# A nanmax over 2048 elements: the first tile's load is split by partitions between two issuing engines

## The chip, the cores and the metric

The kernel runs on one core of one Trainium2 chip. The core has five instruction streams that matter here: TensorE (PE), VectorE (DVE), ScalarE (ACT), GpSimd (POOL) and SyncE (SP), and 16 DMA engines that move data between device memory and the on-chip memory of 128 partitions. Time is device microseconds of one execution; the time of a kernel is the median over its runs. A profile is one more execution, recorded by the hardware profiler.

## The reference

```python
batch, seq, dim = 32, 2048, 2048
x = np.random.randn(batch, seq, dim).astype(np.float32)
mask = np.random.rand(batch, seq, dim) < 0.1
x[mask] = np.nan
...
return np.nanmax(x, axis=axis).astype(np.float32)      # axis = -1
```

There are 65,536 rows of 2048 floats, 512 MiB, and one maximum that ignores NaN is wanted of each row: 256 KiB.

## The kernel before

**The arithmetic.** Only the upper 16 bits of each float are changed. A helper `clean` reads them as a signed integer, doubles it, subtracts 0x7F80 and writes it back as an unsigned one, with negative results clipped to zero (`Relu` on ScalarE, the conversion to uint16 on GpSimd). A NaN becomes a pattern that is negative as a float or nearly zero, a small or negative number becomes about zero, and large numbers keep their order. A plain maximum over the row (`tensor_reduce` on VectorE, f32) is then the maximum without the NaNs, as long as it is large enough, and `decode` undoes the step on the 512 results a partition. A count of results that were too small (`mark`, `total`, one small matmul) decides at the very end whether a slow, general version has to run over everything; for this input it doesn't.

**Tiling.** Each partition holds 512 rows. The free dimension is counted in units of 256 elements (`U`), so a row is 8 units (`ROW`). `TILES` lists the tiles; a tile is a list of loads, and a load is a tuple of steps, all in units. A tile of 64 units is 8 rows on each of 128 partitions: 64 KB a partition, 8 MiB. The first two tiles are one load of 16 units (2 MiB) and one of 48 (6 MiB); then come 50 tiles of one 64-unit load each, and then tiles cut into ever smaller loads and steps for a short end.

**Buffers.** There are three buffers of 64 units (`xts`, `BUFS = 3`); tile number n uses buffer n mod 3. A load may be issued when the last reduction of the tile that had the buffer before is done (`free`). The loads of the first three tiles (`AHEAD = 3`) need no buffer freed and are issued at the head of the program, before the barrier at the end of its setup (lines 273 to 286); all others are issued in the main loop. SyncE issues all loads, in the order of tiles. They carry semaphores from 14 lanes in turn (`LANES`); a load also waits for the one that used its lane before.

**Each step.** ScalarE cleans the first half of a step's columns, GpSimd the second half, both as soon as the step's load has landed. The two count on a shared semaphore (`pair`), so VectorE waits once for both and then reduces the rows that are complete. `order.add` writes every instruction with the waits that it still needs: waits that an earlier one on the same engine implies are left out.

**Order on the engines around the change.** SyncE: the three loads ahead, the barrier, then one load after another, each behind its wait for VectorE. ScalarE: the barrier, a table load, one activation on a single column, then the first halves of the steps. GpSimd: four constants, the barrier, the second halves. VectorE: three memsets, then the reductions. At tile numbers in `SETTLE` GpSimd also marks and decodes the rows finished so far.

Of the kernel before, what the change touches and what calls it, by code (L numbers as in the profile page):

```python
# [10 lines left out]
U = 256  # L11
# [2 lines left out]


TILES = (
    [[(16,)], [(48,)]]
    + [[(64,)]] * 50
# [20 lines left out]
OWN = 46  # L39
PAIRS = 6  # L40
# [4 lines left out]
LANES = 14  # L45

AHEAD = 3

# [154 lines left out]
def kernel(  # L203
# [6 lines left out]
    nc = tc.nc  # L210
    P = nc.NUM_PARTITIONS
# [22 lines left out]
    def sbuf(name, shape, dtype):  # L234
        return nc.alloc_sbuf_tensor(name, shape, dtype).ap()

    small = sbuf("small", [P, LEAD // 4], f32)
    xts = [sbuf(f"xt{i}", [P, WIDE * D], i32) for i in range(BUFS)]
# [9 lines left out]
    order = Order(nc)  # L248
    lanes = [[] for _ in range(LANES)]
    issued = 0  # L250

    def load(to, of, deps, own=False):
        nonlocal issued
        turn = issued % LANES
        issued += 1

        def issue():
            inst = nc.sync.dma_start(out=to, in_=of)  # L258
            if own:
                tc.no_tile_sem_insts.add(inst.ins.name)  # L260
            return inst

        e = order.add("sp", nc.sync, issue, deps + lanes[turn], lane=f"load{turn}", step=16)
        lanes[turn] = [e]
        return e

    def source(gi):
        r = P * rows[0] * gi
        return xr[r : r + P * rows[gi]].rearrange("(p s) d -> p (s d)", p=P)
# [3 lines left out]
    ahead = {}  # L273
    base = 0
    for number in range(AHEAD):
        for at, steps in tiles[number]:
            end = at + sum(steps)
            ahead[number, at] = load(
                xts[number][:, at * U : end * U],
                source(0)[:, (base + at) * U : (base + end) * U],  # L280
                [],
                own=True,
            )
        base += sizes[number]
    tc.close()
    tc.compile()  # L286
# [4 lines left out]
    def act(deps, pair=None, **kw):  # L291
        return order.add(
            "act",
            nc.scalar,
            lambda: nc.scalar.activation(**kw),  # L295
            deps,
            lane=pair,
            joint=pair is not None,
        )
# [4 lines left out]
    def pool(deps, do, pair=None, **kw):  # L304
        return order.add(
            "pool", nc.gpsimd, lambda: do(**kw), deps, lane=pair, joint=pair is not None  # L306
        )

    def decode(add, engine, a, b, deps):
        return add(  # L310
            deps,
            engine.tensor_scalar,
            out=halves[:, a:b],
            in0=halves[:, a:b],
            scalar1=float(INF),
            scalar2=0.5,
            op0=ALU.add,
            op1=ALU.mult,
        )

    def clean(by, span, deps, pair):
        to, of = span.bitcast(u16)[:, 1::2], span.bitcast(i16)[:, 1::2]
        if by == "A":
            return act(
                deps, pair, out=to, in_=of, func=ACT.Relu, bias=float(-INF), scale=2.0
            )
        return pool(
            deps,
            nc.gpsimd.tensor_scalar,
            pair,  # L330
            out=to,
            in0=of,
            scalar1=2.0,
            scalar2=float(-INF),
            op0=ALU.mult,
            op1=ALU.add,
        )

    def mark(to, of, deps):
        return pool(  # L340
            deps,
            nc.gpsimd.tensor_scalar,
            out=to,
            in0=of,
            scalar1=NORMAL,
            scalar2=None,
            op0=ALU.is_lt,
        )

    def total(to, of, deps):  # L350
        return act(deps, out=of, in_=of, func=ACT.Relu, bias=0.0, scale=1.0, accum_out=to)
# [11 lines left out]
    for number, loads in enumerate(tiles):  # L363
        if number in (0, SPLIT):
            gi = int(number == SPLIT)
            s = rows[gi]
            xg = source(gi)
            og = outs[r0 : r0 + P * s].rearrange("(p s) -> p s", p=P)
            stores.append([og, accs[:, first : first + s].bitcast(i32)])
            r0 += P * s  # L370
            base = 0
        xt, before = xts[number % BUFS], free[number % BUFS]
        if number in SETTLE:
            to = sum(sizes[: SETTLE[number]]) // ROW
            e_row = done[to - 1]
            e_low = mark(low[:, settled:to], accs[:, settled:to], [e_row])
            e_settled = decode(pool, nc.gpsimd, settled, to, [e_row, e_low])
            settled = to
        if number == len(tiles) - 1:
            assert settled == rows[0]  # L380
            e_early = total(late[:, 0:1], low, [e_low])
        for at, steps in loads:
            end = at + sum(steps)
            e = ahead.get((number, at))
            if e is None:
                e = load(
                    xt[:, at * U : end * U],
                    xg[:, (base + at) * U : (base + end) * U],
                    before,
                )  # L390
            cleaned = []
            a = taken = at
            for i, n in enumerate(steps):
                pair = "pair_%s_%d_%d" % (*e, i) if number >= OWN else f"pair{number % PAIRS}"
                lo, mid, hi = a * U, a * U + n * U // 2, (a + n) * U
                clean("A", xt[:, lo:mid], [e], pair)
                e_clean = clean("P", xt[:, mid:hi], [e], pair)
                cleaned.append((a, a + n, e_clean))
                a += n
                upto = end if a == end else a // ROW * ROW  # L400
                for lo, hi in segments(taken, upto):
                    row = first + (base + lo) // ROW
                    m = max((hi - lo) // ROW, 1)
                    deps = [e for p, q, e in cleaned if p < hi and q > lo]
                    of = lo * U
                    if row >= S - 2:
                        if len(cells) == 1 and e_rest is None:
                            e_rest = dve(
                                [done[S - 3]],
                                nc.vector.tensor_reduce,  # L410
                                out=accs[:, first : S - 2],
                                in_=parts[:, 0 : s - 2],
                                axis=AX.X,
                                op=ALU.max,
                            )
                        if lo % ROW:
                            of -= 1
                            deps.insert(0, cells[row][1])
                        if hi % ROW:
                            to = xt[:, hi * U - 1 : hi * U].bitcast(f32)  # L420
                        else:
                            to = accs[:, row : row + m]
                    elif gi == 1:
                        nth = 0 if lo % ROW == 0 else nth + 1
                        assert nth < PARTS
                        to = parts[:, row - first : row - first + m, nth : nth + 1]
                        deps.append(e_zero)
                    else:
                        assert lo % ROW == 0 and hi % ROW == 0
                        to = accs[:, row : row + m]  # L430
                    e_max = dve(
                        deps,
                        nc.vector.tensor_reduce,
                        out=to,
                        in_=xt[:, of : hi * U]
                        .bitcast(f32)
                        .rearrange("p (c d) -> p c d", c=m),
                        axis=AX.X,
                        op=ALU.max,
                    )  # L440
                    if hi % ROW == 0:
                        for r in range(row, row + m):
                            done[r] = e_max
                    elif row >= S - 2:
                        cells[row] = (hi * U - 1, e_max)
                taken = max(taken, upto)
        free[number % BUFS] = [e_max]
        base += sizes[number]
        if number in (SPLIT - 1, len(tiles) - 1):
            first += s  # L450
# [4 lines left out]
    e = mark(late[:, rows[1] - 1 :], xt[:, p : q + 1 : q - p].bitcast(f32), [e_p, e_q])  # L455
# [7 lines left out]
    e = decode(dve, nc.vector, S - 2, S, [done[S - 2], done[S - 1]])  # L463
# [3 lines left out]
    for og, bits, deps in stores:  # L467
# [6 lines left out]
                lane="store",  # L474
                step=16,
# [66 lines left out]
```

## Time and profile before

| What | Value |
|---|---|
| median of 3 runs | 1246.35 us (1246.26 to 1246.93) |
| the profiled execution's own time | 1246.26 us |
| its span, first to last instruction | 1244.4 us |
| bytes moved by the load and store queue | 537.14 MB, 432 GB/s over the span |
| bytes read from device memory | 536.87 MB |

The span is shorter than the execution's time by what lies before the first and after the last instruction of the program. In the views below, times are microseconds from the start of the span. PE, DVE, ACT, POOL and SPq are the engines, L258 a line of the kernel (a helper's line where the helper records the instruction), `out<-in` the names of what is written and read, followed by shapes and types. A row of the timeline has the start, the duration, the engine, the instruction, and in brackets the idle time before it and what ended it. A row of the waits has who waited for what: total, number of times, the longest. SPq rows are the issues of loads; the page counts DMA work by queue, as a share of the time of all 16 engines.

### The profile page before, as it was taken

Reading aid. Unit: us, or ns where it says so; the run is one execution under the profiler, and the core shown is the slowest. Engines: PE = TensorE matmul, PEld = TensorE weight load, DVE = VectorE, ACT = ScalarE, POOL = GpSimd, SP = SyncE. Lnnn points to the kernel's source line nnn. Section 1 sums busy time; section 2 is a strip of 40 time slices with the busy share of each in tenths; the row PEclk is TensorE's granted clock in tenths of the full one; section 3 lists DMA queues with packets and bytes.
Section 4 is the critical chain, followed back from the end, with each engine's and each line's share of the span. In section 5 each row is a group of like instructions: output and inputs, shape, how many; then the busy total and the mean of one; then the engine's idle time right before and its main releaser. Section 6 shows DMA issues by size and latency. Waiting matters only on the chain.

```text
span 1244.4 us, 572 instructions
## 1 busy us (share of the span) xinstructions
PE 0.2 (0%) x2; PEld 0.1 (0%) x2; DVE 1105.9 (89%) x136; ACT 603.7 (49%) x131; POOL 606.6 (49%) x138
## 2 busy tenths in 40 slices
PE   0000000000000000000000000000000000000000
PEld 0000000000000000000000000000000000000000
DVE  1789889898898988988989889898898999999999
ACT  3354453553534535445354453544535536545556
POOL 3354453543534535445354453544535536545556
DMA  9999999999999999999999999999999999999999
GB/s 404 438 438 438 438 438 438 419 423 438 438 438 438 438 438 430 415 436 438 438 438 438 438 438 421 421 438 438 438 438 438 438 432 419 443 424 430 429 425 375
DMA packets 14688, 537.14 MB, mean 432 GB/s; under 512 B 1760, under 2 KB 1888, under 8 KB 4704
## 3 DMA queue, kind: packets, MB, share of 16 engines
q1 hardware_dynamic: 14688, 537.14, 99.9%
HBM read 536.87 MB, written 0.26 MB: 432 GB/s over the span
## 4 chain that ended last, share of the span: by engine, by line
DMA 50%; DVE 34%; POOL 14%; SPq 2%; issue 0%; ACT 0%; PE 0%
DMA xt<-in_x_dram 50%; DVE acc L302 33%; POOL xt L306 14%; SPq L258 2%; DVE parts L302 1%; POOL late L306 0%; ACT sums L295 0%; PE sums L460 0%; SPq L95 0%
## 5 line engine op out<-in xcount | busy, mean ns | idle before, releaser
L302 DVE TENSOR_REDUCE acc<-xt 128x8 f32<-128x16384 f32 (+5 forms) x95 | 1059.4, 11186 | 134.0 <-POOL xt L306 133.7
L306 POOL TENSOR_SCALAR xt<-xt 128x8192 uint16<-128x8192 int16 (+11 forms) x125 | 602.7, 4836 | 635.0 <-DMA xt<-in_x_dram 635.0
L295 ACT ACTIVATE xt<-xt 128x8192 uint16<-128x8192 int16 (+11 forms) x125 | 601.5, 4839 | 635.2 <-DMA xt<-in_x_dram 635.2
L302 DVE TENSOR_REDUCE parts<-xt 128x1 f32<-128x2048 f32 (+6 forms) x32 | 42.6, 1410 | 0.0
L302 DVE TENSOR_REDUCE xt<-xt 128x1 f32<-128x768 f32 (+1 forms) x4 | 3.7, 944 | 0.0
L302 DVE MEMSET small<- 128x1 f32 x2 | 0.1, 59 | 3.0 <-PEq L286 3.0
L295 ACT ACT_TABLE_LOAD x1 | 1.3, 1283 | 2.9 <-PEq L286 2.9
L306 POOL TENSOR_SCALAR low<-acc 128x312 f32<-128x312 f32 (+2 forms) x3 | 1.9, 626 | 0.2
L306 POOL TENSOR_SCALAR acc<-acc 128x312 uint16<-128x312 uint16 (+3 forms) x4 | 1.4, 343 | 0.3
L295 ACT ACTIVATE sums<-sums 1x22 f32<-1x22 f32 x1 | 0.1, 140 | 1.1 <-PE sums L460 1.1
L295 ACT ACTIVATE low<-low 128x491 f32<-128x491 f32 x1 | 0.6, 585 | 0.0
L460 PE MATMUL sums<-late,small 128*1 128x22 f32 x2 | 0.2, 200 | 1242.4 <-POOL late L306 1242.4
L306 POOL TENSOR_SCALAR late<-acc 128x19 f32<-128x19 f32 x1 | 0.3, 266 | 0.1
L306 POOL TENSOR_SCALAR late<-xt 128x2 f32<-128x2 f32 x1 | 0.2, 218 | 0.1
L460 PEld LDWEIGHTS sums<-late,small 128*1 128x1 f32 x2 | 0.1, 80 | 1242.4 <-issue 1242.4
L523 POOL MEMSET const-float32-0.0<- 128x1 f32 x1 | 0.1, 99 | 0.2 <-issue 0.2
L295 ACT ACTIVATE small<-small 128x1 f32<-128x1 f32 x1 | 0.2, 203 | 0.0
L302 DVE TENSOR_SCALAR acc<-acc 128x2 uint16<-128x2 uint16 x1 | 0.2, 171 | 0.0
L302 DVE TENSOR_REDUCE acc<-parts 128x19 f32<-128x57 f32 x1 | 0.2, 200 | 0.0
L295 ACT ACTIVATION_READ_ACCUMULATOR low<-low 128x1 f32 x1 | 0.2, 187 | 0.0
L295 ACT ACTIVATION_READ_ACCUMULATOR sums<-sums 1x1 f32 x1 | 0.2, 185 | 0.0
L302 DVE MEMSET parts<- 128x63 f32 x1 | 0.1, 111 | 0.0
(3 smaller groups left out, 0.3 us busy)
## 6 DMA issues: line engine op xcount, KB each, us to landing
xt<-in_x_dram SPq DMA_DIRECT2D x2, 7168.0 KB, 30.9
xt<-in_x_dram SPq DMA_DIRECT2D x2, 6144.0 KB, 24.7
xt<-in_x_dram SPq DMA_DIRECT2D x3, 4096.0 KB, 26.7
xt<-in_x_dram SPq DMA_DIRECT2D x5, 2048.0 KB, 34.4
xt<-in_x_dram SPq DMA_DIRECT2D x2, 5120.0 KB, 23.2
xt<-in_x_dram SPq DMA_DIRECT2D x3, 3072.0 KB, 33.6
xt<-in_x_dram SPq DMA_DIRECT2D x4, 1024.0 KB, 34.9
xt<-in_x_dram SPq DMA_DIRECT2D x9, 384.0 KB, 13.9
```

The lines of the kernel that those rows point to most:

```text
L258: inst = nc.sync.dma_start(out=to, in_=of)
L295: lambda: nc.scalar.activation(**kw),
L302: return order.add("dve", nc.vector, lambda: do(**kw), deps)
L306: "pool", nc.gpsimd, lambda: do(**kw), deps, lane=pair, joint=pair is not None
L460: lambda: nc.tensor.matmul(sums, lhsT=ones, rhs=late, start=True, stop=True),
L523: nc = _bacc.Bacc("TRN2", target_bir_lowering=False, num_devices=1)
```

## The change

The first two tiles of 16 and 48 units become one tile of 64 units with one step. Its load is issued in two instructions: partitions 0 to 15 by ScalarE, on ScalarE's own DMA queue, and partitions 16 to 127 by SyncE, 64 KB a partition in both. The loads of the next two tiles are issued by SyncE with all 128 partitions. `load` takes the issuing engine as an argument, and the list of loads that a step waits for can now hold two. Tile numbers behind the first tile are one lower than before.

```diff
--- before.py
+++ after.py
@@ -14,7 +14,7 @@
 
 
 TILES = (
-    [[(16,)], [(48,)]]
+    [[(64,)]]
     + [[(64,)]] * 50
     + [[(24, 40)], [(24, 40)], [(16, 16, 32)], [(8, 16, 32)], [(8, 16, 32)], [(8, 16, 24)]]
     + [[(16, 24)], [(8, 16, 16)], [(16, 16), (16, 16)], [(8, 8, 16), (8, 16)]]
@@ -45,6 +45,7 @@
 LANES = 14
 
 AHEAD = 3
+CORNER = 16
 
 
 
@@ -249,18 +250,19 @@
     lanes = [[] for _ in range(LANES)]
     issued = 0
 
-    def load(to, of, deps, own=False):
+    def load(to, of, deps, own=False, by="sp"):
         nonlocal issued
         turn = issued % LANES
         issued += 1
+        engine = nc.sync if by == "sp" else nc.scalar
 
         def issue():
-            inst = nc.sync.dma_start(out=to, in_=of)
+            inst = engine.dma_start(out=to, in_=of)
             if own:
                 tc.no_tile_sem_insts.add(inst.ins.name)
             return inst
 
-        e = order.add("sp", nc.sync, issue, deps + lanes[turn], lane=f"load{turn}", step=16)
+        e = order.add(by, engine, issue, deps + lanes[turn], lane=f"load{turn}", step=16)
         lanes[turn] = [e]
         return e
 
@@ -275,12 +277,17 @@
     for number in range(AHEAD):
         for at, steps in tiles[number]:
             end = at + sum(steps)
-            ahead[number, at] = load(
-                xts[number][:, at * U : end * U],
-                source(0)[:, (base + at) * U : (base + end) * U],
-                [],
-                own=True,
-            )
+            cuts = [0, P] if number else [0, CORNER, P]
+            ahead[number, at] = [
+                load(
+                    xts[number][p:q, at * U : end * U],
+                    source(0)[p:q, (base + at) * U : (base + end) * U],
+                    [],
+                    own=True,
+                    by="act" if q == CORNER else "sp",
+                )
+                for p, q in zip(cuts, cuts[1:])
+            ]
         base += sizes[number]
     tc.close()
     tc.compile()
@@ -383,18 +390,20 @@
             end = at + sum(steps)
             e = ahead.get((number, at))
             if e is None:
-                e = load(
-                    xt[:, at * U : end * U],
-                    xg[:, (base + at) * U : (base + end) * U],
-                    before,
-                )
+                e = [
+                    load(
+                        xt[:, at * U : end * U],
+                        xg[:, (base + at) * U : (base + end) * U],
+                        before,
+                    )
+                ]
             cleaned = []
             a = taken = at
             for i, n in enumerate(steps):
-                pair = "pair_%s_%d_%d" % (*e, i) if number >= OWN else f"pair{number % PAIRS}"
+                pair = "pair_%s_%d_%d" % (*e[0], i) if number >= OWN else f"pair{number % PAIRS}"
                 lo, mid, hi = a * U, a * U + n * U // 2, (a + n) * U
-                clean("A", xt[:, lo:mid], [e], pair)
-                e_clean = clean("P", xt[:, mid:hi], [e], pair)
+                clean("A", xt[:, lo:mid], e, pair)
+                e_clean = clean("P", xt[:, mid:hi], e, pair)
                 cleaned.append((a, a + n, e_clean))
                 a += n
                 upto = end if a == end else a // ROW * ROW
```

## The prediction

> **What bounds the kernel now.** I read the span and queue totals on the page first, then the waits, then the first 135 us of the timeline, then stretches of the span, and last the chain of waits at the start.
>
> ```profile
> span 1244.4 us, 572 instructions
> PE 0.2 (0%) x2; PEld 0.1 (0%) x2; DVE 1105.9 (89%) x136; ACT 603.7 (49%) x131; POOL 606.6 (49%) x138
> q1 hardware_dynamic: 14688, 537.14, 99.9%
> ACT xt L295 <- DMA xt<-in_x_dram: 635.2, 96, 12.3
> POOL xt L306 <- DMA xt<-in_x_dram: 635.0, 97, 12.3
> DVE acc L302 <- POOL xt L306: 133.7, 53, 14.6
> ```
>
> The packets of the one load queue fill 99.9% of the span of the 16 DMA engines, and ScalarE and GpSimd wait for loads for half of it. VectorE is next at 89%. The profiled execution took 1246.26 us, 1.86 us more than its span. It is the lowest of the three runs shown, 0.09 us under the median.
>
> The steady part, from the timeline (start, duration, engine, line, operation, idle time before it):
>
> ```profile
> 7.96 2.47 ACT L295 ACTIVATE xt<-xt 128x2048 uint16<-128x2048 int16 x1 [3.55 <-DMA xt<-in_x_dram]
> 22.46 6.99 ACT L295 ACTIVATE xt<-xt 128x6144 uint16<-128x6144 int16 x1 [12.03 <-DMA xt<-in_x_dram]
> 29.52 12.95 DVE L302 TENSOR_REDUCE acc<-xt 128x6 f32<-128x12288 f32 x1 [14.60 <-POOL xt L306]
> 41.79 9.25 ACT L295 ACTIVATE xt<-xt 128x8192 uint16<-128x8192 int16 x1 [12.34 <-DMA xt<-in_x_dram]
> 51.12 17.22 DVE L302 TENSOR_REDUCE acc<-xt 128x8 f32<-128x16384 f32 x1 [8.64 <-POOL xt L306]
> 61.13 9.26 ACT L295 ACTIVATE xt<-xt 128x8192 uint16<-128x8192 int16 x1 [10.09 <-DMA xt<-in_x_dram]
> 70.47 17.22 DVE L302 TENSOR_REDUCE acc<-xt 128x8 f32<-128x16384 f32 x1 [2.14 <-POOL xt L306]
> 80.45 9.27 ACT L295 ACTIVATE xt<-xt 128x8192 uint16<-128x8192 int16 x1 [10.06 <-DMA xt<-in_x_dram]
> 89.79 17.22 DVE L302 TENSOR_REDUCE acc<-xt 128x8 f32<-128x16384 f32 x1 [2.10 <-POOL xt L306]
> ```
>
> ScalarE starts a tile when its load has landed, so its starts are landings: 22.46, 41.79, 61.13, 80.45. They are 19.33 us apart, and each tile is 8 MiB (8,388,608 bytes), so the 16 engines move 434 GB/s, 27.1 GB/s each. A 128-partition load of 64 KB a partition is eight rows to an engine, 2.42 us a row. VectorE needs 17.22 us of each 19.33 and idles for the 2.1 left over: it follows the loads and cannot be what a late load eats into.
>
> Now whether the load stream has a gap anywhere. The columns of these stretches are the stretch and its length, busy time of PE, PEld, DVE, ACT and POOL, clock, DMA share and GB/s:
>
> ```profile
> 0.00:1.70 1.70, 0.00 (x0) 0.00 (x0) 0.00 (x0) 0.00 (x0) 0.19 (x4) 1.00 0.00 0
> 1.70:3.00 1.30, 0.00 (x0) 0.00 (x0) 0.00 (x0) 0.09 (x1) 0.00 (x0) 1.00 1.01 252
> 3.00:7.00 4.00, 0.00 (x0) 0.00 (x0) 0.18 (x3) 1.40 (x2) 0.00 (x0) 1.00 1.04 442
> 60.00:1000.00 940.00, 0.00 (x0) 0.00 (x0) 837.11 (x50) 454.04 (x49) 455.10 (x51) 1.00 1.00 435
> 1100.00:1200.00 100.00, 0.00 (x0) 0.00 (x0) 99.85 (x31) 53.07 (x30) 55.10 (x32) 1.00 1.00 432
> 1230.00:1241.00 11.00, 0.00 (x0) 0.00 (x0) 11.00 (x14) 7.69 (x12) 7.53 (x12) 1.00 1.03 413
> ```
>
> There is none: from 1.7 us to 1241 the engines are full. So what the first tile's load loses or gains arrives at the end unchanged. Near the end VectorE is full as well (99.85 of 100 us), but its work there waits for tiles that would be late by the same amount.
>
> **What the change removes and moves on the compute engines.** Before, tile 0 (16 units, 2 MB) and tile 1 (48 units, 6 MB) lie in two buffers; after, one tile of 64 units lies in one. ScalarE's 2.47 + 6.99 us become one 9.25. The first reduction starts when the whole 8 MiB is clean: 22.46 + 9.3 = 31.8 instead of VectorE's early start in the first half, and ends at 49.0. The next tile is clean at 51.1 as before (41.79 + 9.3), so VectorE is ready for it with 2.1 us to spare, its steady margin. Cost on the path: nothing.
>
> The buffer is the other thing to check, with the chain of waits:
>
> ```profile
> 8.01 2.47 POOL xt L306
> 10.50 4.43 DVE acc L302
> 14.95 46.16 DMA xt<-in_x_dram
> 61.10 0.07 issue
> ```
>
> Before, the fourth load is issued when the 2 MB tile is reduced, at 14.95, and lands at 61.10: nearly all of its 46.16 us is queueing. After, the first load that waits for a buffer is tile 3's, issued at 49.0 behind two 8 MiB loads that last until 61.1; it will land at about 80.5. Cover: 61.1 − 49.0 = 12.1 us. If all of the first tile's load is late, its followers are late too, and the cover stays 12.1. From there on every tile stands as its counterpart does now, since the three buffers turn in the same order. Cost: nothing. Without that cover each microsecond of a late issue would be a microsecond of idle load engines.
>
> Three load instructions of SyncE before the first barrier stay three, and ScalarE gets one, beside them. ScalarE's and GpSimd's first instruction wait for two loads instead of one; ScalarE's other work of that time (table load, one tiny activation) ends long before 22 us. A semaphore wait more, behind which only the first tile's halves queue: nothing. The settling work of GpSimd changes by a few columns (312 to 320), in its idle half: nothing.
>
> **The start of the stream.** Between 1.7 and 3.0 us the engines move 252 GB/s where 435 is their pace: (435 − 252) / 435 × 1.3 = 0.55 us lost, the engines' first packets. A second queue that hands each engine one row could win part of that back; it could also add its own start. Bounds −0.55 to +0.5 us (as much again); I take −0.2.
>
> **The split by partitions.** This is the term that decides. Every load in the trace before covers 128 partitions, and 27.1 GB/s is what one engine does with its eight of them. No row shows a load of 16 or of 112. The corner is 16 rows of 64 KB, one for each engine if it goes to all 16; but all 16 land in 16 neighbouring partitions.
>
> Lower bound: place does not matter, a row is 2.42 us on any engine, 1 + 7 = 8 rows an engine as before. Loss 0.
>
> Upper bound: 16 partitions take in only what the trace shows 16 partitions taking in, two engines' worth, 2 × 27.1 = 54.2 GB/s. The 1,048,576 bytes then take 19.3 us instead of 2.42, and the 16 engines, each holding one such row, are kept from their other rows: loss 16.9 us.
>
> I take the middle, 8.5 us: the trace has neither row, sixteen engines at one eighth of the memory is nearer to the crowded end in shape, but the rows of the big load can fill in where an engine has not reached its corner row. [...]
>
> For the 112 rows, seven to an engine instead of eight: bounds 0 (place does not matter) and 16.9 us (every row meets another one and takes twice 2.42, seven times). I take one such meeting on the engine that ends last, 2.4 us: it is the smallest step that isn't zero, and 112 partitions are nearer in shape to 128 than to 16.
>
> Sum: −0.2 + 8.5 + 2.4 = +10.7 us. 1246.26 + 10.7 = 1257.0 us, 0.9% slower. The landings of the second and third tile would come at about 52.5 and 71.8 instead of 41.79 and 61.13, and everything behind them shifts alike.
>
> [...]
>
> **Rivals.**
>
> 1. Crowding all through. If rows of neighbouring partitions go to neighbouring engines in the big load too, its seven rounds are as crowded as the corner. At a quarter of the pace (between one eighth and one) the whole tile takes 4 × 19.33 = 77.3 us, +58 us: 1304. For it: only the unknown order in which 112 partitions are dealt out. Against it: 14 of 16 eighths of the memory are there to be written.
>
> 2. Less than I take: engines write to each other's partitions at a full 27.1 GB/s except for a short start, loss 1 to 3 us, 1248. For it: engines drift apart by what the start gives them, so meetings break up.
>
> 3. Not slower: place doesn't matter, 1 + 7 rows are eight rows, and the first packets are won back. −0.55 to 0 us, 1246.0. For it: the pace is the same, 442 and 435 GB/s, for short rows and long ones, as it would be if each engine were its own limit. It decides as soon as the corner lands within about 22 us and the second tile at 41.8. For the same time: the corner is late but its engines go on with other rows; a landing up to 12.1 us late would then be hidden, by the cover above.
>
> 4. The change doesn't do what it says: ScalarE's queue starts late, after its table load. ScalarE issues ahead of its first barrier, so against it stands the order of its instructions; it would cost nothing more, since the corner would only come later in the same stream, and is counted with the forecast.
>
> A gain over 2.5 us has no place to come from: before 1.7 us nothing moves and after it only 0.55 us are lost.
>
> **How the numbers follow.** This kernel's runs tell a difference from none at about 0.2%, 2.5 us. Forecast (loss of 4 to 20 us): 0.63. Rival 1: 0.09. Rival 2: 0.06, half of it over 2.5 us. Rival 3: 0.22, with 0.02 for a gain that I don't see. Slower 0.63 + 0.09 + 0.03 = 0.75; same 0.03 + 0.20 = 0.23; faster 0.02. The range starts at rival 3's gain, 1246.26 − 0.55 = 1245.7, and ends at both bounds of the crowding in part, 1246.26 + 16.9 + 2 × 2.4 = 1268: left out are rival 1 and the forecast's far end, some 0.13 together. The forecast's own range is 1250 to 1266.
>
> **What would show it.** A first ScalarE activation of 128x8192 later than 22.5 us, at about 33; the next landing 19.33 us behind that or sooner, and the third load's at 70 to 75 instead of 61.13; GB/s under 400 in the stretch from 3 to 30 us. Right on the compute side if VectorE still idles 2.1 us a tile. Wrong if the first activation of 128x8192 stands at 22.5 and the second at 41.8 (rival 3), or if the first is late and the third is not (the corner held nothing up), or if a gap in the load stream appears at 61 us (the cover was miscounted).

## The result and the profile after

| | before | after |
|---|---|---|
| median | 1246.3 us (5 runs, 1246.26 to 1246.93) | 1268.26 us (5 runs, 1267.4 to 1269.17) |
| span of the profiled execution | 1244.4 us | 1266.5 us |

The change makes the kernel slower: the ratio is 1.0176, 95% interval 1.0162 to 1.019. That is 22.0 us, twice what was forecast, and 0.26 us beyond the end of the range.

From the page of the changed kernel, the span and the two load queues (q10 is ScalarE's):

```profile
span 1266.5 us, 571 instructions
...
q1 hardware_dynamic: 14528, 536.09, 99.0%
q10 hardware_dynamic: 32, 1.05, 0.7%
```

From its timeline, the first three tiles:

```profile
44.92 9.25 ACT L302 ACTIVATE xt<-xt 128x8192 uint16<-128x8192 int16 x1 [40.50 <-DMA xt<-in_x_dram]
...
54.25 17.22 DVE L309 TENSOR_REDUCE acc<-xt 128x8 f32<-128x16384 f32 x1 [51.06 <-POOL xt L313]
64.21 9.26 ACT L302 ACTIVATE xt<-xt 128x8192 uint16<-128x8192 int16 x1 [10.04 <-DMA xt<-in_x_dram]
...
71.50 0.33 SPq L260 DMA_DIRECT2D xt<-in_x_dram  x1
73.55 17.22 DVE L309 TENSOR_REDUCE acc<-xt 128x8 f32<-128x16384 f32 x1 [2.08 <-POOL xt L313]
83.49 9.26 ACT L302 ACTIVATE xt<-xt 128x8192 uint16<-128x8192 int16 x1 [10.02 <-DMA xt<-in_x_dram]
```

The first tile lands at 44.92 instead of 22.46, the next two at 64.21 and 83.49 instead of 41.79 and 61.13: 22.4 us late each, and the span is 22.1 longer. Everything is lost in the first tile's load, and what is lost there arrives at the end. From the second tile on the pace is the old one, 19.3 us a tile, with VectorE idling 2.08.

Stretches of the load (stretch and length, busy time of PE, PEld, DVE, ACT, POOL, clock, DMA share, GB/s):

```profile
3.00:16.00 13.00, 0.00 (x0) 0.00 (x0) 0.18 (x3) 1.41 (x2) 0.00 (x0) 1.00 0.97 136
16.00:41.00 25.00, 0.00 (x0) 0.00 (x0) 0.00 (x0) 0.00 (x0) 0.00 (x0) 1.00 0.92 228
```

The 16 engines are busy nearly all the time (0.97 and 0.92), but move 136 GB/s while the corner's rows are among the work and 228 after it, where 435 was the pace. These views book a row of 64 KB, its bytes and its time, where it starts, so a short stretch is off by the rows at its edges: from 1.7 to 3.0 us of this kernel they give a share of 3.70, where 1 is full. Share and rate together give the mean time that one row was under way: 16 × 0.97 × 65,536 bytes / 136 GB/s = 7.5 us in the first stretch and 4.2 us in the second, against 2.42 in the steady stream. The rows that the two queues started between 5 and 14 us (packets, MB, share of 16 engines) show the corner by itself:

```profile
q10 hardware_dynamic: 16, 1.05, 97.7%
q1 hardware_dynamic: 1, 0.07, 4.2%
```

Its 16 rows take 8.8 us each (97.7% of 9 us on 16 engines), and only one other row starts. But not only the corner is slow: the 112 rows behind it go at about half pace for 25 us.

### The profile page after: what moved, and what is told of

Its sections match the earlier page's. It is cut to its first block, busy times and chain, and to the rows that moved or that the text cites. A ratio compares the mean times of both kernels' runs of the same rounds, so it can differ in the third digit from the quotient of the medians.

```text
span 1266.5 us, 571 instructions
## 1 busy us (share of the span) xinstructions
PE 0.2 (0%) x2; PEld 0.1 (0%) x2; DVE 1105.7 (87%) x135; ACT 603.5 (48%) x130; POOL 606.4 (48%) x137
## 4 chain that ended last, share of the span: by engine, by line
DMA 49%; DVE 31%; POOL 15%; SPq 3%; another core or an unknown queue 2%; issue 0%; ACT 0%; PE 0%
DMA xt<-in_x_dram 49%; DVE acc L309 31%; POOL xt L313 15%; SPq L260 3%; ACT sums L302 0%; PE sums L469 0%; POOL late L313 0%; DVE xt L309 0%; SPq L96 0%
## 5 line engine op out<-in xcount | busy, mean ns | idle before, releaser
L309 DVE TENSOR_REDUCE acc<-xt 128x8 f32<-128x16384 f32 (+6 forms) x94 | 1059.3, 11305 | 156.3 <-POOL xt L313 156.1
L313 POOL TENSOR_SCALAR xt<-xt 128x8192 uint16<-128x8192 int16 (+12 forms) x124 | 602.5, 4873 | 657.4 <-DMA xt<-in_x_dram 657.4
L302 ACT ACTIVATE xt<-xt 128x8192 uint16<-128x8192 int16 (+12 forms) x124 | 601.3, 4876 | 657.7 <-DMA xt<-in_x_dram 657.6
```

The source lines that it names most:

```text
L309: return order.add("dve", nc.vector, lambda: do(**kw), deps)
```

## The experiments

Edits are shown against the changed kernel. In the first four the question is which part of the change costs.

**One load.** The merged tile, without the split:

```diff
-            cuts = [0, P] if number else [0, CORNER, P]
+            cuts = [0, P]
```

> The first tile stays one tile of 64 units, but its load is one instruction of SyncE with all 128 partitions. Split theory (the loss lies in loads of fewer than 128 partitions): first clean of ScalarE at 22.5 us, 1246.0 to 1246.6 us. Rival (the merged tile itself costs, through a late buffer or a late first reduction): the first clean at 22.5 us all the same, but 1250 to 1268 us.

Measured: 1246.7 us, ratio to before 1.0002 (0.9992 to 1.0011). From its timeline, the first two tiles:

```profile
22.92 9.25 ACT L302 ACTIVATE xt<-xt 128x8192 uint16<-128x8192 int16 x1 [18.51 <-DMA xt<-in_x_dram]
...
42.23 9.27 ACT L302 ACTIVATE xt<-xt 128x8192 uint16<-128x8192 int16 x1 [10.06 <-DMA xt<-in_x_dram]
```

The merge of the two tiles, the late first reduction and the later release of the first buffer cost nothing that can be told. All 22 us belong to the split.

**One queue.** Both parts from SyncE, the 112 partitions first:

```diff
-                    by="act" if q == CORNER else "sp",
+                    by="sp",
...
-                for p, q in zip(cuts, cuts[1:])
+                for p, q in reversed(list(zip(cuts, cuts[1:])))
```

> Both loads of the first tile are issued by SyncE, the 112 partitions first, then the 16. Split theory: as slow as the change, 1265 to 1270 us, with 200 to 230 GB/s from 3 to 30 us while only the 112 rows are under way and some 110 GB/s behind them for the corner. Rival (two queues on the same engines get in each other's way): 1246 to 1252 us.

Measured: 1268.78 us, ratio 1.0181 (1.0164 to 1.0198). The second queue is not what costs. Since the parts now follow each other, two stretches of this kernel separate them:

```profile
3.00:30.00 27.00, 0.00 (x0) 0.00 (x0) 0.19 (x3) 1.49 (x2) 0.00 (x0) 1.00 0.93 233
32.00:40.00 8.00, 0.00 (x0) 0.00 (x0) 0.00 (x0) 0.00 (x0) 0.00 (x0) 1.00 0.87 131
```

The 112 rows by themselves run at 233 GB/s, then the corner, mixed with the first rows behind it, at 131.

**Split by columns.** ScalarE issues 1 MiB as before, but 8 units of all 128 partitions (`CUT = 8` replaces `CORNER`):

```diff
-            cuts = [0, P] if number else [0, CORNER, P]
+            cuts = [at, end] if number else [at, CUT, end]
...
-                    xts[number][p:q, at * U : end * U],
-                    source(0)[p:q, (base + at) * U : (base + end) * U],
+                    xts[number][:, p * U : q * U],
+                    source(0)[:, (base + p) * U : (base + q) * U],
...
-                    by="act" if q == CORNER else "sp",
+                    by="act" if q == CUT else "sp",
```

> The first tile's load is split by columns instead of partitions: ScalarE issues the first 8 units of all 128 partitions (1 MiB, as much as the corner), SyncE the other 56 units. Split theory: no loss, 1245.8 to 1246.8 us. Rival (two queues): 1250 us or more.

Measured: 1246.61 us, ratio 1.0002 (0.9992 to 1.0012). Two queues with 128 partitions each lose nothing, and gain nothing at the start either.

**Near source.** The rows of the first tile lie side by side in device memory:

```diff
+    near = xr[0 : P * WIDE].rearrange("(p s) d -> p (s d)", p=P)
...
-                    source(0)[p:q, (base + at) * U : (base + end) * U],
+                    (source(0) if number else near)[p:q, (base + at) * U : (base + end) * U],
```

> The change with its two loads, but both read rows that lie one behind the other in device memory (partitions 64 KB apart instead of 4.02 MB); it reads other rows for the first tile, so those results are of other rows. Theory that the loss lies where the rows land: unchanged, 1266 to 1270 us. Rival (the addresses that are read together get in each other's way): 1246 to 1256 us.

Measured in one run: 1266.92 us. With the addresses that are read quite different the loss is still there, which points away from the reading side and to where the rows land.

**Ten shapes.** Which sets of partitions are slow? Loads one after another, each issued when the one before has landed:

```diff
-AHEAD = 3
+AHEAD = 0
...
+PROBES = (
...
+    done_probe = []
+    for part in PROBES:
+        done_probe = [
+            load(xts[0][part, 0 : 64 * U], source(0)[part, 0 : 64 * U], done_probe)
+        ]
...
-    free = [[] for _ in range(BUFS)]
+    free = [done_probe for _ in range(BUFS)]
```

> Ahead of its normal work (first tile in one load, no loads ahead of the barrier) this kernel loads ten shapes into the first buffer, 64 KB a partition, each when the one before has landed: partitions 0-127, 16-127, 0-111, 0-63, 64-127, 0-31, 0-15, then 16 partitions 8 apart, 32 partitions 4 apart, and 0-95. Its own time is not of interest. Each load's duration is to be read, about 2.1 us of which are fixed. Theory that where rows land sets the pace (neighbouring partitions share a way in, so the same number of rows goes faster when spread): 16 neighbours take 9.7 + 2 us, 16 partitions 8 apart half of that; 0-63 takes 15 to 20 us, 112 rows 29 us. Rival (how many rows an engine has is all that counts in a load by itself): 19.3, 16.9, 16.9, 9.7, 9.7, 4.8, 2.4, 2.4, 4.8, 14.5 us, each + 2. Second rival (any load of other than 128 partitions is slow, wherever it lands): 16 spread partitions as slow as 16 neighbours.

The chain of waits of this kernel is the loads themselves, in the order listed (start, duration from issue to landing):

```profile
1.48 22.32 DMA xt<-in_x_dram
...
23.82 33.24 DMA xt<-in_x_dram
...
57.08 32.73 DMA xt<-in_x_dram
...
89.83 23.00 DMA xt<-in_x_dram
...
112.85 22.87 DMA xt<-in_x_dram
...
135.74 12.22 DMA xt<-in_x_dram
...
147.97 11.39 DMA xt<-in_x_dram
...
159.37 7.38 DMA xt<-in_x_dram
...
166.77 7.62 DMA xt<-in_x_dram
...
174.40 31.89 DMA xt<-in_x_dram
```

128 partitions take 22.32 us, 3.0 more than their 19.33 in the stream; that, and not the 2.1 of the expectation, is taken as the fixed part. The rest, against rows per engine times 2.42 us:

| partitions | measured − 3.0 | if only rows counted |
|---|---|---|
| 16-127 and 0-111 | 30.2 and 29.7 | 16.9 |
| 0-63 and 64-127 | 20.0 and 19.9 | 9.7 |
| 0-31 | 9.2 | 4.8 |
| 0-15 | 8.4 | 2.4 |
| 16, 8 apart | 4.4 | 2.4 |
| 32, 4 apart | 4.6 | 4.8 |
| 0-95 | 28.9 | 14.5 |

Sixteen neighbours go at under a third of the pace, 32, 64, 96 or 112 at about half, and 32 partitions spread over the whole memory at full pace. Both rivals fall: the number of rows doesn't explain it, nor does "fewer than 128", since 32 rows are fast when spread. 112 rows take longer than 128, 33.24 and 32.73 us against 22.32.

**Halves.** The cut at 64 (`CORNER = 64`):

> The change with the cut at 64 instead of 16: ScalarE issues partitions 0 to 63, SyncE 64 to 127, 4 MiB each, four rows to an engine in each. Theory that each half of the partitions takes in half the pace: if the 16 engines work on the same half at the same time, 8 rows at twice 2.42 us: 38.7 instead of 19.3, 1263 to 1267 us. Rival (only the corner's 16 partitions are crowded, 64 are enough): 1246 to 1252 us.

Measured in one run: 1266.16 us, 19.9 us more than the 1246.3 of before, and as the theory has it. The rows that started in two stretches, 6.5 to 11.2 and 11.2 to 16 us (packets, MB, share of 16 engines; q10 has the load of partitions 0 to 63, q1 that of 64 to 127):

```profile
q10 hardware_dynamic: 15, 0.98, 96.9%
...
q1 hardware_dynamic: 16, 1.05, 101.1%
```

The two loads do not run side by side on half of the engines each: all 16 take a row of one load and then a row of the other, so that in these stretches they crowd into one half of the memory at a time.

**Spread parts.** Four loads of 32 partitions 4 apart, one of them by ScalarE:

```diff
-            cuts = [0, P] if number else [0, CORNER, P]
+            cuts = [slice(0, P)] if number else [slice(p, P, 4) for p in range(4)]
...
-                    xts[number][p:q, at * U : end * U],
-                    source(0)[p:q, (base + at) * U : (base + end) * U],
+                    xts[number][part, at * U : end * U],
+                    source(0)[part, (base + at) * U : (base + end) * U],
...
-                    by="act" if q == CORNER else "sp",
+                    by="act" if number == 0 and part == cuts[0] else "sp",
...
-                for p, q in zip(cuts, cuts[1:])
+                for part in cuts
```

> The first tile's load is again split by partitions and by issuing engine, but every part is spread over all of them: ScalarE issues partitions 0, 4, 8 ... 124, SyncE three more loads of 32 partitions 4 apart, beginning at 1, 2 and 3. Theory that neighbours crowd: no crowding, first tile lands at 22 to 24.5 us, 1246.3 to 1249 us. Rival (any load of fewer than 128 partitions is slow, or several loads of one tile are): first tile at 35 us or later, 1259 us or more.

Measured: 1247.25 us, ratio 1.0006 (0.9997 to 1.0016). The first row of ScalarE's cleaning in its timeline:

```profile
23.29 9.25 ACT L302 ACTIVATE xt<-xt 128x8192 uint16<-128x8192 int16 x1 [17.19 <-DMA xt<-in_x_dram]
```

A split by partitions into four loads on two queues, and the 22 us are gone: it is neighbours that cost, not the split.

**Sixteens.** The other end, eight loads of 16 neighbours (`slice(p, p + 16) for p in range(0, P, 16)` in the same edit):

> The first tile's load in eight loads of 16 neighbouring partitions each, the first by ScalarE, seven by SyncE: the corner eight times over. Theory that neighbours crowd: each round of 16 rows takes what the corner's takes, 9.6 us, so 8 x 9.6 = 77 us, or down to 48 us where the engines have drifted apart far enough to work in two of the eighths at once; 1275 to 1304 us. Rival (the loss comes from the corner's other queue and the cut of 112, not from 16 neighbours): no slower than the change, 1268 us.

Measured in one run: 1301.04 us. One stretch, and the first tile:

```profile
22.00:60.00 38.00, 0.00 (x0) 0.00 (x0) 0.00 (x0) 0.00 (x0) 0.00 (x0) 1.00 0.98 110
...
77.54 9.25 ACT L302 ACTIVATE xt<-xt 128x8192 uint16<-128x8192 int16 x1 [70.35 <-DMA xt<-in_x_dram]
```

The pace is 110 GB/s, a quarter of 435, and the tile lands 54.6 us later than in one load. Full, half, quarter: 1247, 1266 and 1301 us for the same bytes.

**Nine more shapes**, to see what "neighbour" means (the edit of the ten shapes with another list):

> The kernel with ten loads ahead of its work, now with nine others: 64 partitions 2 apart, 32 partitions 2 apart (0-62), 48 partitions 2 apart (0-94), 32 partitions 3 apart (0-93), 8 partitions 16 apart, 8 partitions 4 apart (0-28), 8 neighbours (0-7), partitions 0-119, 0-127. Each takes about 3 us beside its rows, by the load of 128 partitions in the run before. Theory: four neighbours share one way in, and so does the group 32 further; the other half of the memory has ways of its own, 16 in all, each at 27 GB/s. Then 64 partitions 2 apart have all 16 ways: 9.7 + 3 us; 32 partitions 2 apart within one half have 8: 9.7 + 3; 8 partitions 16 apart have 4: 4.8 + 3; 8 partitions 4 apart have 8: 2.4 + 3; 8 neighbours have 2: 9.7 + 3. For 48 partitions and for 120 the theory has no number without the order in which rows are dealt to engines; half pace as with 96 would be 14.5 + 3 and 36 + 3 us. Rival (the distance between the first and the last partition sets the pace, not groups of four): 8 partitions 16 apart faster than 8 partitions 4 apart.

```profile
1.49 12.84 DMA xt<-in_x_dram
...
14.35 12.80 DMA xt<-in_x_dram
...
27.17 16.77 DMA xt<-in_x_dram
...
43.95 12.20 DMA xt<-in_x_dram
...
56.16 7.45 DMA xt<-in_x_dram
...
63.63 5.18 DMA xt<-in_x_dram
...
68.83 11.14 DMA xt<-in_x_dram
...
79.98 42.48 DMA xt<-in_x_dram
...
122.48 22.35 DMA xt<-in_x_dram
```

Four of the predicted ones came as predicted: 64 partitions 2 apart 12.84 (full pace), 32 within one half 12.80 (half), 8 partitions 16 apart 7.45, 8 partitions 4 apart 5.18. The 8 neighbours took 11.14 instead of 12.7, and 0-127 took 22.35, as in the ten shapes. The distance rival falls: rows 16 apart are slower than rows 4 apart, 7.45 us against 5.18, as they would be if 0 and 32, or 16 and 48, share. The first two also speak against the reading side once more: their rows are equally far apart in device memory, and one load goes at twice the pace of the other.

The three without a firm number were all at about half pace: 48 in 16.77, 32 partitions 3 apart in 12.20, and 0-119 in 42.48, nearly twice what 128 take. The load of 120 has a second handicap. The rows that start in its first 4 us, and in the first 4 us of the load of 16-127 in the ten shapes (packets, MB, share of 16 engines):

```profile
q1 hardware_dynamic: 15, 0.98, 111.0%
...
q1 hardware_dynamic: 16, 1.05, 102.4%
```

Only 15 rows of the 120 start together, against 16 of the 112. If all rounds are like the first, which alone was counted, that is eight rounds of 15 rows instead of seven rounds of 16, an estimate.

**Own way or shared way.** That 112 rows are slow on every engine could also mean that an engine writes only its own group at full pace:

> The kernel with loads ahead of its work, now small ones in which no two rows share a group of partitions, but the groups are shifted against the engines: 8 partitions 4 apart beginning at 0, at 4 and at 64; 4 partitions 4 apart beginning at 0 and at 16; 4 partitions 8 apart; 4 neighbours (0-3); 32 partitions 4 apart; 16 partitions 4 apart from 4 to 64. Theory that only sharing a way costs: all of the first six take 2.4 us for the row and about 2.8 us beside it, 5.2 us; the 4 neighbours, all on one way, 9.7 + 2.8 us. Second theory (each engine has one way of its own, which it writes at full pace, and crosses to any other at half pace, shared or not): 8 from 0 and 4 from 0 take 5.2 us, all others of the first six 4.8 + 2.8 = 7.6 us. The 112 rows, slowed on every engine, would follow from the second theory and not from the first.

```profile
1.48 5.16 DMA xt<-in_x_dram
...
6.66 5.06 DMA xt<-in_x_dram
...
11.73 5.09 DMA xt<-in_x_dram
...
16.84 5.10 DMA xt<-in_x_dram
...
21.96 5.12 DMA xt<-in_x_dram
...
27.10 5.06 DMA xt<-in_x_dram
...
32.18 11.39 DMA xt<-in_x_dram
...
43.58 7.99 DMA xt<-in_x_dram
...
51.59 7.72 DMA xt<-in_x_dram
```

All six sets without sharing take 5.06 to 5.16 us, shifted or not; four neighbours take 11.39, a little less than the 12.5 expected. The last two had no number beforehand: 32 partitions 4 apart, two rows to an engine, take 7.99, and 16 partitions from 4 to 64, most of which would share two by two, 7.72. The second theory falls: in these loads of one row to an engine only neighbours cost, 11.39 us against at most 5.16. That also takes away the theory from which the slowness of the 112 rows would have followed; for them, sharing in every round remains an inference.

**One corner too many**, to price the corner inside the stream. The first tile in one load, and 16 rows more into the second buffer, which the second tile's load then overwrites:

```diff
-AHEAD = 3
+AHEAD = 1
...
+    part = slice(0, CORNER)
+    extra = load(
+        xts[1][part, 0 : 64 * U], source(0)[part, 64 * U : 128 * U], [], own=True, by="act"
+    )
...
-            cuts = [0, P] if number else [0, CORNER, P]
+            cuts = [0, P]
...
-    free = [[] for _ in range(BUFS)]
+    free = [[], [extra], []]
```

> The first tile in one load of 128 partitions by SyncE, as in the first run; in addition ScalarE loads 16 rows of 64 KB into partitions 0 to 15 of the second buffer, which the second tile's load, issued behind it, writes again: 1 MiB more than needed, to price the corner by itself inside the stream. Beside the 1246.7 us of one load, theory that neighbours crowd: the 16 engines are held for the 8.4 to 9.3 us that such rows take by themselves and in eights, 1255 to 1256 us. Rival (in the stream the other rows fill in): only the bytes count, 2.4 us, 1249.1 us. My price for it in the prediction was 8.5 us over the bytes, which would be 1257.6 us.

**The same bytes, spread** (`slice(0, P, P // CORNER)`):

> The same 1 MiB too much, into 16 partitions 8 apart instead of 16 neighbours. Theory that neighbours crowd: such partitions share a way two by two, 4.8 us, 1251 to 1252 us, half the price of the neighbours. Rival (only the bytes count): 1249.1 us, as for the neighbours.

Measured in one run each: 1256.64 and 1251.92 us. The first row of cleaning in the first and in the second:

```profile
33.01 9.25 ACT L306 ACTIVATE xt<-xt 128x8192 uint16<-128x8192 int16 x1 [29.56 <-DMA xt<-in_x_dram]
```

```profile
28.30 9.25 ACT L306 ACTIVATE xt<-xt 128x8192 uint16<-128x8192 int16 x1 [24.42 <-DMA xt<-in_x_dram]
```

Beside 1246.7 for one load the neighbours cost 9.9 us and the spread rows 5.2, both for the same 1 MiB; 2.4 would be its share at full pace. So the corner costs 9.9 − 2.4 = 7.5 us over its bytes.

## Why the prediction was half right

**Compute side and buffers: right.** One load of the merged tile takes 1246.7 us. The cover foretold as 12.1 us is there although everything moved: tile 3's load is issued at 71.50 and the engines have work until 83.49, 12.0 us.

**That a loss at the start arrives nearly whole at the end: right.** 22.4 us in the first three landings, 22.1 in the span.

**The start of the stream, −0.2 us: not seen.** The split by columns also gives each engine work from a second queue, and its ratio is 1.0002, with no gain that can be told. The 0.55 us behind the term came from a stretch of 1.3 us in which bytes are booked where rows start (its first 0.1 us shows 1147 GB/s), so its size was loose too.

**The corner, +8.5 us: right in kind and nearly in size.** Measured 7.5 in the stream. That the size is so near is partly luck: 8.5 was the middle between no loss and 16.9, not worked out from a mechanism. That it matters which partitions are written together is what the small shapes show: 4 neighbours take 11.39 us against 5.10 for 4 partitions 4 apart, and 8 partitions 16 apart, which would share two by two in the theory of the nine shapes, 7.45 against 5.18 for 8 partitions 4 apart. That theory does not price the larger loads: in it partitions 0 to 95 and 0 to 111 have all the ways in that 128 have, and they took 31.89 and 32.73 us, about half pace. There the measurement decides.

**The 112 rows, +2.4 us: the step that failed.** Its row was counted as "one such meeting on the engine that ends last", because "112 partitions are nearer in shape to 128 than to 16". In pace they are like 64 or 32: 30.2 us against 16.9 by rows, where 0-63 takes 20.0 against 9.7 and 0-31 takes 9.2 against 4.8. The load by itself takes 30.2 us instead of 16.9, which is +13.3, near the upper bound of 16.9 that the same step had stated. In the kernel 22.0 − 7.5 = 14.5 us are left for it, by subtraction. With that in place of 2.4 the sum would have been −0.2 + 8.5 + 14.5 = +22.8, 1269.1 us. The range took in the corner's bound in full and this one only at 2 × 2.4, and so fell short by 0.26 us.

**The rivals.** "Crowding all through" at a quarter of the pace (1304) is what eight sixteens do (1301.04); 112 rows do it at about half, 228 GB/s of 435. The argument against that rival counted wrongly: 112 partitions are seven of eight eighths of the memory, not "14 of 16 eighths"; and that nearly all of the memory was there to be written did not help. "Not slower", which would have needed place not to matter, fell with the ten shapes, and again with the cut into two halves, which cost 19.9 us. That ScalarE's queue would start late is not what decides: from one queue the time is the same, 1268.78 us against 1268.26.

**What stays open.** Which engine gets which of 112 rows: no run here shows it. The half pace of 48, 96, 112 and 120 partitions, and of 32 partitions 3 apart, fits a dealing in which engines meet two by two at nearly every row, but that was inferred from the pace. So that the 112 rows run at half pace is measured; why they do is not shown. Nor is why four rows that share a way in the theory take 8.1 us (8 neighbours) to 8.4 (4 neighbours) beside the fixed 3.0, where four times 2.42 is 9.7, and why 16 neighbours take 8.4 us by themselves and 9.9 in the stream.

## What to carry to other kernels

What was measured here, with rows of 64 KB: keep loads at 128 partitions (1246.7 us), and where one has to be cut, cut its columns (1246.61 us), or take partitions 4 apart over the whole memory (1247.25 us), not a block of neighbours (1268.26 us with the cut at 16, 1266.16 at 64). The small loads say that what counts is where the rows that are under way at one moment land, not how many partitions the load has: 16 neighbours took 11.39 us, 16 partitions 8 apart 7.38. A load that leaves out an eighth of the partitions took nearly 50% longer than one of all of them, 33.24 us against 22.32, so a partial load is not priced by its bytes. And where a term of a prediction rests on no row at all, the far end of its bounds belongs in the range.

## What was not expected of the hardware

112 partitions take 33.24 us, 128 take 22.32 and 120 take 42.48: fewer rows, more time. The 120 began with 15 rows in 4 us, the 112 with 16. 32 partitions 3 apart (0 to 93) take 12.20 us, 32 partitions 4 apart (0 to 124) 7.62. In the busy shares of the changed kernel nothing of this shows: while the load ran at a third to a half of its pace, 136 and 228 GB/s of 435, the share of the 16 engines stood at 0.92 to 0.97. A row counts as busy for as long as it is under way, 7.5 or 4.2 us where it would need 2.42.
